# A convolution worked by halves: channel tile 7 moved from ScalarE and GpSimd to TensorE and VectorE, two row spreads merged, and two more filling matmuls

## The chip, the cores and the metric

The kernel runs on one core of a Trainium2 chip. A core has TensorE (PE in the profile) for matrix products, VectorE (DVE), ScalarE (ACT) and GpSimd (POOL) for elementwise work, and SyncE (SP), whose queue issues the DMA transfers. The metric is the device time of one execution in microseconds (us); lower is better. Three runs of the kernel before took 1380.88, 1380.84 and 1377.91 us, the median is 1380.84.

## The reference

Four layers work on x of 256 positions by 1024 channels (float32). Each adds a mixer and then a squared-ReLU MLP, both behind an RMS norm. The mixers are retention (layers 0 and 3), a convolution module (layer 1) and stick-breaking attention (layer 2). The change lies mostly in the convolution module:

```python
def conformer_conv_mixer(xn, pw1_w, pw1_b, dw_w, dw_b, ln_w, ln_b, pw2_w, pw2_b):
    h = xn @ pw1_w + pw1_b
    a, gate = jnp.split(h, 2, axis=-1)
    h = a * jax.nn.sigmoid(gate)
    h = lax.conv_general_dilated(          # depthwise, 31 taps, causal
        h, dw_w[:, None, :].astype(h.dtype), window_strides=(1,),
        padding=[(CONV_WIDTH - 1, 0)],
        dimension_numbers=('NWC', 'WIO', 'NWC'),
        feature_group_count=D_MODEL) + dw_b
    h = layer_norm(h, ln_w, ln_b)
    h = jax.nn.silu(h).astype(xn.dtype)
    return h @ pw2_w + pw2_b

for i in range(DEPTH):                      # DEPTH = 4
    h = rms_norm(x, norm_mix[i])
    x = x + mixer_i(h)
    x = x + squared_relu_mlp(rms_norm(x, norm_ffn[i]), ffn_w1[i], ffn_w2[i])
return rms_norm(x, final_norm)
```

## The kernel before

**Products.** Channels lie on the 128 partitions, positions along the free axis. A float32 product is made of three products of rounded values: every weight unit (128x1024) is loaded by SP into a raw buffer (L334), cast by ACT to its high part `wh` (L346), and VectorE subtracts to get the low part `wl` (L347). Activations are split in the same way. `mm_b` (L484 to L486), `mm_w` (L511, L512) and L552, L553 then multiply high by high, high by low and low by high. Outside the stretches named below a scheduler orders the instructions of each engine.

**Start.** `warm(9)` (L291) issues nine 128x512 matmuls on a tile of ones while the first weights are on their way. The first real matmul is L552, in retention.

**RMS norm.** The squares of four x tiles are added on GpSimd (L447). `norm_r` (L452ff) then lets GpSimd add the two halves of that sum (L455) into a new tile, TensorE sums over the channels (L393), VectorE makes a reciprocal root `r` in a chain of small operations (L377 to L388), and TensorE broadcasts it (L400).

**The convolution** (`conv`, L907ff). After pw1 and the gate, `hc[0..7]` holds the eight channel tiles, each 256 positions behind 31 zeros. The 31 taps of a tile are done in one of three ways:

- tile 0 on VectorE (`tap_dve`, L1004: one multiply-add per tap, into two accumulators that take turns, which lie in PSUM);
- tile 1 on ACT (a scaled copy, L1011) and GpSimd (an add, L1013);
- tiles 2 to 6 (`PET`) on TensorE. `spread` (L925) writes a tile's rows to DRAM (`hd`, L928) and reads them back (L931) so that four shifted copies of 32 channels fill the partitions. `taps_pe` (L1015) then needs 32 matmuls per tile and half, against diagonal weight strips that GpSimd prepares (L918). `spread(2)` and `spread(4)` move two tiles each, `spread(6, 1)` one.

Tile 7 is split by positions: its first half (`taps_7a`) is done on VectorE with accumulators in PSUM, its second half (`taps_7b`) on ACT and GpSimd.

From here the order on TensorE, VectorE, ACT and GpSimd is written out by hand (L1165 to L1250). A "half" h is 128 of the 256 positions. For each half: `fin_pe` (L1119) takes the convolution out of PSUM and subtracts a shift `Gb`, `square` (L1027) squares it on ACT, `stats` (L1035) sums over channels on TensorE, four tiles at a time; `cols_st` (L393), `mean_in`, `mean_out` (L410) and `scale_in` (a reciprocal root, L1058 to L388), `scale_out` (L410) make mean and scale; `swish_mean` (L1131), `swish` (L1136, then ACT's Silu, L1141 and L1142) normalise. The second product, pw2, has two parts. Channel tiles 0 to 3 are multiplied with unsplit weights `W` (L356 loads them, `mm_h`, L1159) half by half; tiles 4 to 7 are kept as high and low parts `y` (low part: L1146) and go through `mm_b` at the end. Then the MLP starts with L511.

On SP's queue the order around this is: the two spreads of tiles 2 to 5, the eight loads of `W` (L356, 256 KB each), the spread of tile 6 (L928, L931), and the loads of the next weights (L334), which wait for a raw buffer.

## Time and profile before

| | before |
|---|---|
| runs (us) | 1380.88, 1380.84, 1377.91; median 1380.84 |
| the profiled execution (us) | 1379.88, of which the span from first to last instruction is 1378.1 |
| granted TensorE clock, mean | 0.997 |
| TensorE busy | 1359.6 us (99%), weight loads 1233.6 us (90%) |
| VectorE, ScalarE, GpSimd busy | 985.8 us (72%), 784.1 us (57%), 146.3 us (11%) |
| DMA | 239.29 MB, mean 174 GB/s |

The profile is of one execution. A timeline row gives the start, the time from the first instruction's start to the last one's end, engine, line, operation, out<-in, the count, and in brackets the idle time before it and what ended it. Matmuls overlap, so the time from one matmul's start to the next one's is shorter than the time of one. A row of the waits gives, for what TensorE was about to start and what it waited for, total us, times, and the longest. A row of the windows gives busy time and count for each engine, then the granted clock as a share of full speed.

### The profile page before, as it was taken

The page shows a single profiled execution, that of the slowest core. Times are in us where ns is not written, and L with a number is a line of the kernel's source. Part 1 is how long each engine was busy: PE and PEld are TensorE (multiplying, and loading weights), DVE is VectorE, ACT ScalarE, POOL GpSimd, SP SyncE. Part 2 cuts the span into 40 slices and gives each one's busy share as a digit, 9 for nine tenths or more (in the row PEclk, how much of TensorE's full clock was granted, in tenths as well). Part 3 has the DMA queues.
Part 4 walks back from the last instruction along what each step waited for, and adds up shares of the span by engine and source line. Part 5 has one row for each costly group of instructions (what it writes and reads, how often), then busy time and mean ns, then how long its engine had stood idle before and what let it go on. Part 6 is the DMA issues. An engine that isn't in the chain of part 4 may idle for free.

```text
span 1378.1 us, 23268 instructions
## 1 busy us (share of the span) xinstructions
PE 1359.6 (99%) x9339; PEld 1233.6 (90%) x9339; DVE 985.8 (72%) x1709; ACT 784.1 (57%) x1203; POOL 146.3 (11%) x154
## 2 busy tenths in 40 slices
PE   9999999999999899999999999999999999999998
PEld 8889998888999798888988898888988999988888
DVE  6967778775679678765578587755597687788643
ACT  7555556664447567654468666644565554555442
POOL 2201003000218310000000010000120010100011
PEclk9999999999999999999999999999999999999999
DMA  7644446555556345555543345555454444455550
GB/s 288 217 153 154 153 154 214 184 184 187 180 184 158 128 148 195 189 190 188 187 157 123 137 169 184 186 190 199 171 181 175 153 154 165 173 191 190 190 190 34
DMA packets 38860, 239.29 MB, mean 174 GB/s; under 512 B 4320, under 2 KB 8160, under 8 KB 11360
## 3 DMA queue, kind: packets, MB, share of 16 engines
q1 hardware_dynamic: 38464, 237.28, 49.1%
q8 instruction: 73, 1.20, 0.3%
q10 hardware_dynamic: 288, 0.52, 0.1%
q14 instruction: 35, 0.29, 0.1%
HBM read 236.01 MB, written 1.78 MB: 173 GB/s over the span
## 4 chain that ended last, share of the span: by engine, by line
PE 94%; DVE 3%; ACT 2%; issue 1%; POOL 0%; DMA 0%; SPq 0%; ACTq 0%; DVEq 0%; POOLq 0%
PE acc L511 32%; PE acc L512 16%; PE acc L486 8%; PE acc L484 8%; PE acc L485 8%; PE acc L903 4%; PE acc L902 4%; PE acc L904 4%; DVE mis L1004 1%; PE acc L1159 1%; PE mis L393 1%; PE acc L500 1%; PE acc L498 1%; PE acc L499 1%; PE mis L400 1%; PE mis L799 1%
## 5 line engine op out<-in xcount | busy, mean ns | idle before, releaser
L347 DVE TENSOR_TENSOR wl<-raw,wh 128x1024 fp32r<-128x1024 f32 (+1 forms) x440 | 544.5, 1240 | 285.8 <-ACT wh L346 282.0
L346 ACT CAST wh<-raw 128x1024 fp32r<-128x1024 f32 (+1 forms) x440 | 456.7, 1041 | 422.2 <-PE acc L511 206.3
L511 PE MATMUL acc<-z,wh 128*128 128x512 f32 x1120 | 392.0, 395 | 0.0
L512 PE MATMUL acc<-z,wl 128*128 128x256 f32 x1120 | 312.9, 281 | 0.0
L511 PE MATMUL acc<-big,wh 128*128 128x512 f32 x768 | 269.0, 395 | 0.0
L511 PEld LDWEIGHTS acc<-z,wh 128*128 128x128 f32 x1120 | 209.4, 188 | 48.0
L512 PE MATMUL acc<-big,wl 128*128 128x256 f32 x768 | 215.4, 280 | 0.0
L512 PEld LDWEIGHTS acc<-z,wl 128*128 128x128 f32 x1120 | 211.5, 189 | 0.8
L511 PEld LDWEIGHTS acc<-big,wh 128*128 128x128 f32 x768 | 144.0, 187 | 33.8
L486 PE MATMUL acc<-big,wl 128*128 128x256 f32 x544 | 153.5, 283 | 0.0
L485 PE MATMUL acc<-big,wh 128*128 128x256 f32 x544 | 153.3, 283 | 0.0
L484 PE MATMUL acc<-big,wh 128*128 128x256 f32 x544 | 153.1, 284 | 0.0
L484 PE MATMUL acc<-z,wh 128*128 128x256 f32 x512 | 146.1, 286 | 0.0
L486 PE MATMUL acc<-z,wl 128*128 128x256 f32 x512 | 145.9, 285 | 0.0
L485 PE MATMUL acc<-z,wh 128*128 128x256 f32 x512 | 145.7, 285 | 0.0
L512 PEld LDWEIGHTS acc<-big,wl 128*128 128x128 f32 x768 | 145.1, 189 | 0.0
L447 POOL TENSOR_TENSOR t<-t,t 128x512 f32<-128x512 f32 x25 | 38.4, 1534 | 748.1 <-DVE z L432 458.8
L485 PEld LDWEIGHTS acc<-big,wh 128*128 128x128 f32 x544 | 104.2, 192 | 0.0
L486 PEld LDWEIGHTS acc<-big,wl 128*128 128x128 f32 x544 | 104.2, 192 | 0.0
L484 PEld LDWEIGHTS acc<-big,wh 128*128 128x128 f32 x544 | 103.6, 192 | 0.5 <-issue 0.3
L486 PEld LDWEIGHTS acc<-z,wl 128*128 128x128 f32 x512 | 98.8, 193 | 0.0
L484 PEld LDWEIGHTS acc<-z,wh 128*128 128x128 f32 x512 | 98.8, 193 | 0.0
(253 smaller groups left out, 1901.7 us busy)
## 6 DMA issues: line engine op xcount, KB each, us to landing
raw<-in_w SPq DMA_DIRECT2D x214, 1024.0 KB, 4.8
raw<-in_w SPq DMA_DIRECT2D x8, 512.0 KB, 8.0
raw<-hd SPq DMA_DIRECT2D x8, 263.0 KB, 4.7
x<-in_x SPq DMA_DIRECT2D x4, 256.0 KB, 6.3
big<-in_w SPq DMA_DIRECT2D x4, 256.0 KB, 6.2
t<-in_w SPq DMA_DIRECT2D x4, 256.0 KB, 7.6
cst<-in_cst SPq DMA_DIRECT2D x4, 192.0 KB, 5.0
hd<-big SPq DMA_DIRECT2D x5, 143.5 KB, 1.9
```

The lines of the kernel that those rows point to most:

```text
L346: nc.scalar.copy(hi[:, s], src[:, s])
L347: nc.vector.tensor_sub(lo[:, s], src[:, s], hi[:, s])
L393: return self.nc.tensor.matmul(dst, src, sc, start=start, stop=stop, skip_group_check=True)
L447: (nc.vector if p == 3 and self.quick else nc.gpsimd).tensor_add(a, self.sq, q)
L484: nc.tensor.matmul(o, wh[:, kk, cs], ah, start=st, stop=False, **kw)
L485: nc.tensor.matmul(o, wh[:, kk, cs], al, start=False, stop=False, **kw)
L486: nc.tensor.matmul(o, wl[:, kk, cs], ah, start=False, stop=en, **kw)
L511: nc.tensor.matmul(ps[m], wh[:, kk, cs], a, start=first and kk == 0, stop=False, **kw)
L512: nc.tensor.matmul(ps[m][:, :S], wl[:, kk, cs], a[:, :S], start=False, stop=last and kk == 3, **kw)
L902: nc.tensor.matmul(ps[t], zh[:, s], wh[:, kk], start=k == 0, stop=False, skip_group_check=True)
L903: nc.tensor.matmul(ps[t], zh[:, s], wl[:, kk], start=False, stop=False, skip_group_check=True)
L904: nc.tensor.matmul(ps[t], zl[:, s], wh[:, kk], start=False, stop=k == 7, skip_group_check=True)
```

## The change

1. `warm(9)` becomes `warm(11)`.
2. `norm_r` with `halves` adds in place instead of into a new tile. The scheduler places that add by itself.
3. `PET` takes tile 7 in. Tile 7's first half is done by `taps_pe(7, 0)` on TensorE, its second half by VectorE (`taps_7`, all 31 taps), with both accumulators in SBUF. ACT and GpSimd do no taps of tile 7 any more; GpSimd makes two more weight strips.
4. `spread` always moves two tiles: tiles 6 and 7 share one. The loads of `W` are issued behind that spread.
5. Hand order: `taps_pe(6, 0)` and `(7, 0)` stand behind `(3, 1)`; `shift_bb` stands one tile of taps later.
6. Mean and scale of both halves go into one tile each (`lnb`, `lnr`), so that tiles 4 to 7 are normalised once at full width, at the end (`swish_hl`), and no longer by halves.

The diff, cut to its core:

```diff
-PET = (2, 3, 4, 5, 6)
+PET = (2, 3, 4, 5, 6, 7)
...
-        self.warm(9)
+        self.warm(11)
...
         if halves:
-            sq, n = self.tmp(S), 1
-            nc.gpsimd.tensor_add(sq, self.sq[:, :S], self.sq[:, S:])
+            sq, n = sq[:, :S], 1
+            nc.gpsimd.tensor_add(sq, sq, self.sq[:, S:])
...
-        spread(6, 1)
+        sp = spread(6)
...
-        r7 = halves(self.mis(), P), halves(self.bigt(), P)
+        r7 = halves(self.bigt(), P)
...
-        def taps_7a(ws):
-            for w in ws:
-                tap_dve(7, w, r7[0][w % 2], w < 2, w == 0, 0)
-
-        def taps_7b(ws):
-            for w in ws:
-                tap_pool(7, w, r7[1][w % 2], w < 2, w == 0, 1)
...
+        def taps_7(ws):
+            for w in ws:
+                tap_dve(7, w, r7[w % 2], w < 2, w == 0, 1)
...
+        def swish_hl(*ds):
+            def hi(d):
+                y[d] = self.bigt(F32R)
+                return y[d][:, :S]
+
+            a = slice(0, S)
+            swish(a, ds[0], fn=hi)
             for d, e in zip(ds, ds[1:] + (None,)):
                 if e is not None:
-                    begin(e)
-                end(d)
+                    swish(a, e, fn=hi)
+                nc.vector.tensor_sub(y[d][:, S:], cc[d][:, a], y[d][:, a])
...
-            W = [self.unit_raw(key(0, p), [(self.tmp if p < 2 else self.bigt)() for _ in range(2)]) for p in range(4)]
             taps_pe(2, 0)
             shift_a()
...
             shift_c()
-            fin_pe(0, 2, 3, 4)
+            with self.tc.issue_after(sp.ins):
+                W = [self.unit_raw(key(0, p), [(self.tmp if p < 2 else self.bigt)() for _ in range(2)]) for p in range(4)]
+            fin_pe(0, 2, 3)
...
             taps_pe(6, 0)
+            taps_7(range(24, CW))
             fin_pe(0, 6)
+            taps_pe(7, 0)
+            fin_7()
+            fin_pe(0, 7)
             taps_pe(4, 1, range(4))
             stats(0, 4, 5, 6, 7)
...
-            swish_mean(0, 4, 5, 6, 7)
             fin_pe(1, 6)
-            swish(0, 4, 5)
...
-            swish(0, 6, 7)
...
             for p in range(4):
                 mm_h(p, range(4), 1)
-            swish_mean(1, 4, 5, 6, 7)
-            swish(1, 4, 5, 6, 7)
+            swish_mean(slice(0, S), 4, 5, 6, 7)
+            swish_hl(4, 5, 6, 7)
```

Where instructions move, by engine. A row is line, operation, out<-in, shape and what the instruction waits for; "x15" says that it stands so often.

GpSimd in the first retention layer, before. L447 are the adds of the squares, L455 is `norm_r`'s add, L727 fills a score tile after the Activation it waits for:

```order
L447 TENSOR_TENSOR t_33_269<-t_31_265,t_32_267 128x512 [waits Activation_49,Pool_49]
L727 TENSOR_TENSOR big_255<-t_37_278 128x256 [waits Activation_49]
L727 TENSOR_TENSOR big_356<-t_48_351 128x256 [waits Activation_49]
L727 TENSOR_TENSOR big_356<-t_60_425 128x256 [waits Activation_49]
L455 TENSOR_TENSOR t_74_504<-t_33_269 128x256 [waits DVE_49,Pool_49]
```

The same place after the change (line numbers are lower by one):

```order
L446 TENSOR_TENSOR t_33_271<-t_31_267,t_32_269 128x512 [waits Activation_49,Pool_49]
L454 TENSOR_TENSOR t_33_271<-t_33_271 128x256 [waits Pool_49]
L726 TENSOR_TENSOR big_257<-t_37_280 128x256 [waits Activation_49]
L726 TENSOR_TENSOR big_358<-t_48_353 128x256 [waits Activation_49]
L726 TENSOR_TENSOR big_358<-t_60_427 128x256 [waits Activation_49]
```

The add has moved ahead of three others, and it waits for GpSimd's own last add only, no longer for VectorE, which used to release the new tile.

TensorE in the convolution, before, from `taps_pe(3, 1)` to the second four tiles of `stats` of half 0 (`acc_4883` to `acc_4886` are the PSUM tiles, `raw_4865` holds the spread rows of tile 6, `cst` the ones for the sum):

```order
L1017 MATMUL acc_4884<-raw_4837,big_4282 32x128 x16
L1017 MATMUL acc_4883<-raw_4865,big_4292 32x128 [waits DMAHW6_49,DMAHW5_49,DMAHW7_49,DMAHW4_49,DVE_49]
L1017 MATMUL acc_4883<-raw_4865,big_4292 32x128 x15
L1017 MATMUL acc_4883<-raw_4865,big_4294 32x128 x16
L1017 MATMUL acc_4885<-raw_4845,big_4284 32x128 x16
L1035 MATMUL mis_5277<-big_4875,cst 32x256
L1035 MATMUL mis_5277<-big_4876,cst 32x256 [waits Activation_49]
L1035 MATMUL mis_5277<-big_4877,cst 32x256 [waits Activation_49]
L1035 MATMUL mis_5277<-big_4878,cst 32x256
```

And after (`raw_4870` holds the rows of tiles 6 and 7):

```order
L1017 MATMUL acc_4888<-raw_4841,big_4282 32x128 x16
L1017 MATMUL acc_4887<-raw_4870,big_4292 32x128 [waits DMAHW6_49,DMAHW5_49,DMAHW7_49,DMAHW0_49,DVE_49]
L1017 MATMUL acc_4887<-raw_4870,big_4292 32x128 x15
L1017 MATMUL acc_4887<-raw_4870,big_4294 32x128 x16
L1017 MATMUL acc_4888<-raw_4870,big_4296 32x128 [waits DVE_49]
L1017 MATMUL acc_4888<-raw_4870,big_4296 32x128 x15
L1017 MATMUL acc_4888<-raw_4870,big_4298 32x128 x16
L1017 MATMUL acc_4889<-raw_4849,big_4284 32x128 x16
L1036 MATMUL mis_5235<-big_4880,cst 32x256
L1036 MATMUL mis_5235<-big_4881,cst 32x256 [waits Activation_49]
L1036 MATMUL mis_5235<-big_4882,cst 32x256 [waits Activation_49]
L1036 MATMUL mis_5235<-big_4883,cst 32x256 [waits Activation_49]
```

32 matmuls for tile 7's first half stand between the taps of tile 6 and the sums; the sums still wait for ACT's squares of tiles 5, 6 and 7.

VectorE at the end of the convolution, before, behind the multiplications of half 1's first four tiles by its scale (`lnr`):

```order
L1136 TENSOR_TENSOR big_4874<-big_4874,lnr_963_5654 128x128 [waits DVE_49]
L347 TENSOR_TENSOR wl_5675<-raw_5622,wh_5674 128x1024 [waits Activation_49]
L1131 TENSOR_TENSOR big_4875<-big_4875,lnb_952_5606 128x128
L1131 TENSOR_TENSOR big_4878<-big_4878,lnb_952_5606 128x128 [waits Pool_49]
L347 TENSOR_TENSOR wl_5804<-raw_5801,wh_5803 128x1024 [waits DMAHW1_49,Activation_49]
L1136 TENSOR_TENSOR big_4875<-big_4875,lnr_963_5654 128x128 [waits DVE_49]
L347 TENSOR_TENSOR wl_5844<-raw_5801,wh_5843 128x1024 [waits Activation_49]
L347 TENSOR_TENSOR wl_5888<-raw_5885,wh_5887 128x1024 [waits DMAHW2_49,Activation_49]
L1146 TENSOR_TENSOR big_5573<-big_4875,big_5573 128x128 [waits Activation_49]
```

And after, from the same multiplication to the low part of tile 4 (L1146):

```order
L1127 TENSOR_TENSOR big_4879<-big_4879,lnr_4892 128x128 [waits DVE_49,Activation_49]
L347 TENSOR_TENSOR wl_5591<-raw_5588,wh_5590 128x1024 [waits DMAHW1_49,Activation_49]
L1121 TENSOR_TENSOR big_4880<-big_4880,lnb_4891 128x256
L1121 TENSOR_TENSOR big_4883<-big_4883,lnb_4891 128x256
L347 TENSOR_TENSOR wl_5686<-raw_5588,wh_5685 128x1024 [waits Activation_49]
L1127 TENSOR_TENSOR big_4880<-big_4880,lnr_4892 128x256 [waits DVE_49]
L347 TENSOR_TENSOR wl_5728<-raw_5725,wh_5727 128x1024 [waits DMAHW2_49,Activation_49]
L1127 TENSOR_TENSOR big_4881<-big_4881,lnr_4892 128x256 [waits DVE_49]
L347 TENSOR_TENSOR wl_5768<-raw_5725,wh_5767 128x1024 [waits Activation_49]
L347 TENSOR_TENSOR wl_5812<-raw_5809,wh_5811 128x1024 [waits DMAHW3_49,Activation_49]
L1146 TENSOR_TENSOR big_5631<-big_4880,big_5631 128x256 [waits Activation_49]
```

(The two middle L1131 and the two middle L1121 rows are left out.) Tiles 4 to 7 now pass at 256 columns, once, and five weight splits instead of four stand between the last scale and the first low part.

116 lines of the change are left out of this document (49 added, 67 removed).

## The prediction, before the run

> **What bounds the kernel now.** The page comes first: the span, the busy shares, and the chain that ended last.
>
> ```profile
> span 1378.1 us, 23268 instructions
> PE 1359.6 (99%) x9339; PEld 1233.6 (90%) x9339; DVE 985.8 (72%) x1709; ACT 784.1 (57%) x1203; POOL 146.3 (11%) x154
> PE 94%; DVE 3%; ACT 2%; issue 1%; POOL 0%; DMA 0%; SPq 0%; ACTq 0%; DVEq 0%; POOLq 0%
> ```
>
> TensorE is the path: 94% of the chain lies on it. So time is won only where TensorE waits, runs at a lower clock, or has less to do, and each matmul that is added costs its own length. The second view is therefore everything that TensorE waited for, over the whole run (what it was about to start, what it waited for, us in total, times, the longest).
>
> ```profile
> PE mis L1035 <- ACT big L1027: 3.5, 2, 2.3
> PE acc L1159 <- ACT big L1142: 1.9, 1, 1.9
> PE mis L393 <- POOL t L455: 1.6, 1, 1.6
> PE acc L1017 <- DMA raw<-hd: 1.4, 1, 1.4
> PE mis L291 <- POOL ones L269: 1.3, 1, 1.3
> PE acc L552 <- ACT wh L346: 0.9, 1, 0.9
> PE mis L400 <- DVE lns L1085: 0.8, 1, 0.8
> PE mis L410 <- DVE vy L388: 0.6, 1, 0.6
> PE acc L1017 <- issue: 0.3, 1, 0.3
> ```
>
> The list is short, and the change touches nearly all of it. Six rows belong to the convolution: 3.5 + 1.9 + 1.4 + 0.8 + 0.6 + 0.3 = 8.5 us. One belongs to `norm_r` (1.6), one to the start (0.9). Nothing else in 1378 us waits, so whatever is won early is carried to the end: no wait on other engines is there to take it back, unless a new one arises.
>
> The third view is the clock, in windows around the long waits.
>
> ```profile
> 40.00:60.00 20.00, 18.40 (x133) 17.82 (x132) 20.00 (x33) 10.48 (x17) 6.23 (x5) 0.91 0.54 189
> 44.00:48.00 4.00, 4.00 (x23) 4.00 (x22) 4.00 (x6) 2.27 (x4) 1.40 (x2) 0.58 0.76 295
> 480.00:490.00 10.00, 8.11 (x58) 7.91 (x57) 6.45 (x21) 7.92 (x14) 0.00 (x0) 0.83 0.15 43
> ```
>
> The seventh figure of a row, behind the five busy times, is the granted clock. Of 4 us at 0.58, (1 - 0.58) x 4 = 1.7 us of clock are missing; of 10 us at 0.83, also 1.7. At half clock that is 3.4 us each, once behind the 1.6 us wait for L455 and once behind the 1.9 us wait for L1142. So each of these two waits cost its own length and 1.7 us more.
>
> **Start: two more fillers.** The timeline of TensorE, and ACT's cast of the second weights:
>
> ```profile
> 1.29 4.02 PE L291 MATMUL mis<-ones 128*128 128x512 bf16 x9 [1.29 <-POOL ones L269]
> 6.24 1.22 PE L552 MATMUL acc<-z,wh 128*128 128x512 f32 x2 [0.92 <-ACT wh L346]
> 8.96 1.05 PE L552 MATMUL acc<-z,wh 128*128 128x512 f32 x2
> 11.07 0.62 PE L552 MATMUL acc<-z,wh 128*128 128x512 f32 x2
> 13.86 0.63 PE L552 MATMUL acc<-z,wh 128*128 128x512 f32 x2
> 9.36 1.14 ACT L346 CAST wh<-raw 128x512 fp32r<-128x512 f32 x2 [0.64 <-DMA raw<-in_w]
> ```
>
> A filler takes 4.02 / 9 = 0.45 us. Two take 0.9 and end at 5.31 + 0.9 = 6.2, where the first cast ends: the 0.92 us of idle cover them. If that cover were shorter in some run, they would cost up to 0.9.
>
> What they may bring is the clock. A group of products takes 8.96 - 6.24 = 2.7 us at first and (13.86 - 11.07) / 2 = 1.4 later, so full clock came between 8.96 and 11.07. If it is granted in a fixed beat of 3.4 us, then counting ten beats back from the drop near 44.6 (44.6 - 34.1) gives 10.5 for that moment, and the beat before began at 7.1. The idle 0.92 us lies in the beat from 3.7 to 7.1; with it filled, full clock should come at 7.1. Then the weights bound: their cast starts at 9.36, its first half is there at 9.36 + 0.57 = 9.9, and the group at 11.07 can start 1.1 us earlier. I take 1.1; ends: -0.9 (late first matmul), +1.7 (a whole beat).
>
> **The norm's add.** GpSimd did it at 41.84; the sums follow, and much later the root is broadcast:
>
> ```profile
> 41.84 1.57 POOL L455 TENSOR_TENSOR t<-t 128x256 f32<-128x256 f32 x1 [3.10 <-DVE big L740]
> 43.47 0.61 PE L393 MATMUL mis<-cst,t 128*128 128x1 f32 x4 [1.60 <-POOL t L455]
> 65.28 0.16 DVE L388 SCALAR_TENSOR_TENSOR ry<-rt,ry 128x2 f32<-128x2 f32 x1
> 68.99 0.60 PE L400 MATMUL mis<-cst,ry 128*128 128x128 f32 x4
> ```
>
> GpSimd stood idle 3.10 us before the add: what released it was VectorE (L740), since the new tile's old content had to be read first. In place, and placed behind the last add of squares, it needs neither, and TensorE finds it done. The wait (1.6) and the half-clock stretch (1.7) go: 3.3 us. What is late next is VectorE, which is busy in all 20.00 of 20 us from 40 to 60 and can't come forward with TensorE. Its root ends at 65.44, TensorE uses it at 68.99: a margin of 3.55 us, against 1.1 + 3.3 = 4.4 wanted. VectorE gains part of the first 1.1 itself, so I lose a third of a microsecond: 3.0. Ends: 0 (VectorE gives all of it back) and 3.5.
>
> **The convolution.** The stretch runs from the first taps to the start of pw2's second part (L484), which is unchanged itself.
>
> ```profile
> 441.52 1.96 PE L1017 MATMUL acc<-raw,big 128*32 128x128 f32 x64
> 457.25 2.84 PE L1017 MATMUL acc<-raw,big 128*32 128x128 f32 x96 [1.43 <-DMA raw<-hd]
> 489.34 3.74 PE L1159 MATMUL acc<-big,big 128*128 128x128 f32 x32
> 492.83 0.72 PE L484 MATMUL acc<-big,wh 128*128 128x256 f32 x4
> ```
>
> It lasts 492.83 - 441.52 = 51.3 us. Less 8.5 of waits and 1.7 of clock, 41.1 are work and the refilling of the pipeline behind waits, Two rows of taps give both prices: 96 records in 2.84 and 64 in 1.96, so (2.84 - 1.96) / 32 = 0.0275 a record, and 0.2 from the last start to its end, which I take, as an estimate, for the refill behind each of seven waits. Added is one half of a tile: 32 matmuls, 64 records, 1.8 us. Sums, broadcasts and L1159 keep their number. So the work is 41.1 - 1.0 + 1.8 = 41.9, if five of the seven refills go. Which waits stay?
>
> *Tile 6's rows* (1.4) and the W loads. SP's queue, and three rows of the page on DMA (the last figure is the median from issue to landing):
>
> ```profile
> 445.14 0.33 SPq L928 DMA_DIRECT2D hd<-big  x1
> 451.65 1.75 SPq L931 DMA_DIRECT2D raw<-hd  x4
> raw<-hd SPq DMA_DIRECT2D x8, 263.0 KB, 4.7
> t<-in_w SPq DMA_DIRECT2D x4, 256.0 KB, 7.6
> hd<-big SPq DMA_DIRECT2D x5, 143.5 KB, 1.9
> ```
>
> The row write was issued at 445.14, behind the W loads, and the read back only at 451.65, 6.5 us later; the write's usual time is 1.9. With W behind, the writes go out as the gate's last product ends (L953, below: 443.82 + 0.87 = 444.7), the read back near 446.6 to 448.4, and the rows land by 453. TensorE reaches tile 6 after six halves (10.6) and 1.5 of sums and broadcasts, near 453.6. Moved past on SP's queue are two writes and four reads; W then goes out from about 448 and lands by 461, while the first L1159 comes near 466. This wait goes, with 5 us to spare for W.
>
> *The shift* (0.8 and the 0.3 next to it): its broadcast stands a tile of taps later, 1.8 us against 1.1. Gone.
>
> *The squares of half 0's second four* (2.35): VectorE was the slow one, with 31 taps of tile 7 on the way to tile 7's square.
>
> ```profile
> 453.49 2.70 DVE L1004 SCALAR_TENSOR_TENSOR mis<-big,prm,mis 128x128 f32<-128x128 f32 x7
> 456.10 0.35 DVE L1119 SCALAR_TENSOR_TENSOR big<-acc,prm,Gb 128x128 f32<-128x128 f32 x1
> 469.23 0.60 DVE L1119 SCALAR_TENSOR_TENSOR big<-acc,prm,Gb 128x128 f32<-128x128 f32 x2
> 443.82 0.87 DVE L953 SCALAR_TENSOR_TENSOR big<-t,prm,t 128x256 f32<-128x256 f32 x2
> ```
>
> A tap in PSUM takes (456.10 - 453.49) / 7 = 0.37 to 0.39 us. No row shows one of this width with both operands in SBUF: L1119, one in PSUM, stands at 0.30 or less a piece, and the SBUF form at 256 columns at 0.87 / 2 = 0.43, so 0.26 to 0.30. I take 0.28, next to L1119, the row of the same width. From the shift, ready near 448.5, VectorE owes seven L1119 (2.1), tile 0 (0.8), 25 taps (7.0) and tile 7's finish (0.6): 459.0; ACT's square adds 0.4. TensorE gets there after 1.8 us more taps, near 458.4. About 1.0 us of wait stays. With taps at 0.39 it would be 3.8.
>
> *Half 1's squares* (1.1) wait for tile 5 alone now, not for ACT's taps: 0.3 stays. *The root's broadcast* (0.6) sits behind VectorE's chain with GpSimd silent: gone.
>
> *The swish* (1.9): ACT's swish of tiles 0 to 3 of half 1 no longer stands behind those of tiles 6 and 7. Gone, and the 1.7 of clock with it.
>
> *A new wait.* The low part of tile 4 now stands on VectorE behind five weight splits.
>
> ```profile
> 478.73 1.23 DVE L347 TENSOR_TENSOR wl<-raw,wh 128x1024 fp32r<-128x1024 f32 x1 [0.39 <-ACT wh L346]
> 479.87 0.89 DVE L1131 TENSOR_TENSOR big<-big,lnb 128x128 f32<-128x128 f32 x4
> ```
>
> From the scale of half 1 VectorE owes four L1136 like these (0.9), five splits (5 x 1.15 from start to start), four subtractions and two multiplications of double width (6 x 0.35), one low part and its waits for ACT's two swishes of tile 4: about 10 to 11.5. TensorE owes rather more than half of pw2's first part, (492.83 - 489.34) / 32 a record: 5.75 of the eight groups of 16, 92 records, 10.0, and the first four L484, 0.5. I put a wait of 0.8 there, between 0 and 1.3.
>
> So the stretch is 41.9 + 1.0 + 0.3 = 43.2, with the new wait 44.0; before 51.3. That is 7.3. Counted instruction by instruction along TensorE's new order, with taps at 1.76 a half, the same stretch is some 1.5 shorter, since waits let me count too much as work. I take 8.0, between 4.5 (slow taps, 1.3 behind L1146) and 9.5.
>
> **The clock gate.** The rows above show half clock after idle times of 1.6 and 1.9 us, and none after 1.4 and 2.35: length alone doesn't decide. I count no drop behind the waits that stay, of 1.0 or less. [...]
>
> **Sum.** 1.1 + 3.0 + 8.0 = 12.1. The profiled execution took 1379.88, so 1367.8; it lies 0.96 below the median of 1380.84, so against that median 1368.7, say 1368.5. A measurement of this kernel can tell about 0.3%, 4.1 us, from no change.
>
> **Rivals.**
>
> - *Taps no faster in SBUF.* Each tap reads the accumulator written two taps before; if that sets the pace, 0.39 stays. For it: PSUM taps run at 0.37 to 0.39 though L1119 takes 0.30. Against: the SBUF rows. The wait for the squares becomes 3.8: 1371.3. Chance 0.12.
> - *VectorE takes the norm's gain back.* For it: 20.00 busy of 20. Against: the margin of 3.55. Then 1371.5. Chance 0.12.
> - *The two drops of the clock stay*, as something other than the gaps makes them: +3.4, 1371.9. Against: both follow a gap at once, and no other is on record in the middle of the run. Chance 0.04.
> - *The waits only move.* VectorE's part is as long as before, TensorE has 1.8 more to do, and the norm's gain is lost: 1380.84 + 1.8 - 1.1, near 1381. Against: two of the waits, the rows (1.4) and the swish (1.9), have a cause of their own that goes. Chance 0.05.
> - *W late, slower.* Place: the first L1159. The loads of W are behind the spread, and stand in line with the next weights. Each microsecond that W lands after 466 costs one; it undoes the gain at 12.1 late and is 0.3% slower at 16.2, so with a landing near 482, 34 us after issue. They needed 7.6. Chance 0.02.
> - *All waits gone* and a better start: 1363.5. Chance 0.05.
>
> **How the numbers follow.** The forecast has 0.60, on its own 1365 to 1371.5. The range has to take in the first three rivals and the full gain: 1363 to 1374. Faster by more than 0.3% (below 1376.7): 0.60 + 0.12 + 0.12 + 0.04 + 0.05 = 0.93. Within: 0.05. Slower: 0.02.
>
> **What would show it.** In the changed kernel's waits, no row for the norm's add, none for raw<-hd, none for L1142's successor; a row of about 1.0 for the sums behind ACT's square, one near 0.8 at L484 or L485. Windows from 44 to 48 and around the end of the convolution at 1.00; the third group of the start near 10.0. The taps on VectorE at 0.28 from start to start. From the first taps to the first matmul of pw2's second part, about 43. I am wrong if the time is over 1374: then either VectorE sets the pace (waits on VectorE between 45 and 70, or a square wait over 3), or W does.

## The result and the profile after

The changed kernel takes 1369.46 us (median of 4 runs, 1369.21 to 1372.64) against 1380.86 before (4 runs, 1377.91 to 1381.38). The ratio is 0.9927, 95% interval 0.9907 to 0.9947: 11.4 us less. The forecast was 1368.5, with a range of 1363 to 1374. The profiled execution took 1369.21, its span is 1367.4 against 1378.1: 10.7 us less.

The page of the changed kernel, first the span and the busy times, then one row of the DMA queues that will matter:

```profile
span 1367.4 us, 23303 instructions
PE 1354.1 (99%) x9405; PEld 1227.7 (90%) x9405; DVE 983.8 (72%) x1698; ACT 771.1 (56%) x1164; POOL 138.3 (10%) x125
...
q8 instruction: 73, 1.20, 0.3%
```

What TensorE waited for, over the whole run (columns as before; "issue" is time in which the engine waited for nothing that the profile shows):

```profile
PE acc L1017 <- issue: 2.0, 2, 1.7
PE mis L291 <- POOL ones L269: 1.3, 1, 1.3
PE acc L1017 <- DVE big L1004: 1.2, 1, 1.2
PE acc L484 <- DVE big L1146: 1.1, 1, 1.1
PE acc L551 <- ACT wh L346: 1.1, 2, 0.7
PE acc L510 <- DVE z L431: 0.8, 2, 0.4
```

Of the nine rows of before, the norm's add, the swish, the squares, the shift and the root are gone. Two that the forecast struck out are there in a new shape: the stop called issue has grown from 0.3 to 2.0, and there is 1.2 ahead of tile 6. The windows around the old long waits, now at full clock (the seventh figure):

```profile
40.00:60.00 20.00, 20.00 (x145) 18.93 (x144) 20.00 (x35) 11.67 (x18) 5.92 (x4) 1.00 0.52 184
44.00:48.00 4.00, 4.00 (x36) 4.00 (x35) 4.00 (x8) 1.78 (x3) 1.03 (x1) 1.00 0.72 287
480.00:490.00 10.00, 8.86 (x75) 8.65 (x74) 5.28 (x10) 4.10 (x7) 0.00 (x0) 1.00 0.59 211
```

From here the run is cut at three landmarks in the timeline: the first taps, the first L484 product (`mm_b` of pw2; L483 after the change) and the first product of the MLP behind it.

| us | before | after | gained |
|---|---|---|---|
| start to first taps | 441.52 | 437.38 | 4.14 |
| first taps to `mm_b` | 51.31 | 44.24 | 7.07 |
| `mm_b` to the MLP | 11.61 | 12.99 | -1.38 |
| MLP to the end of the span | 873.62 | 872.82 | 0.80 |
| span | 1378.06 | 1367.43 | 10.63 |

**Start and norm.** The timeline of TensorE: the fillers, the first, third and fifth group of products, and the broadcast of the root:

```profile
1.30 4.87 PE L291 MATMUL mis<-ones 128*128 128x512 bf16 x11 [1.30 <-POOL ones L269]
6.52 0.73 PE L551 MATMUL acc<-z,wh 128*128 128x512 f32 x2 [0.35 <-ACT wh L346]
...
10.29 0.73 PE L551 MATMUL acc<-z,wh 128*128 128x512 f32 x2 [0.70 <-ACT wh L346]
...
13.17 0.63 PE L551 MATMUL acc<-z,wh 128*128 128x512 f32 x2
...
64.72 0.66 PE L400 MATMUL mis<-cst,ry 128*128 128x128 f32 x4
```

The third group starts 0.8 earlier (11.07 before), held by the cast, as the 0.70 in brackets says. GpSimd's add now follows its last add of squares at once:

```profile
28.11 1.84 POOL L446 TENSOR_TENSOR t<-t,t 128x512 f32<-128x512 f32 x1 [0.40 <-ACT t L441]
30.03 1.61 POOL L454 TENSOR_TENSOR t<-t 128x256 f32<-128x256 f32 x1
```

It is done at 31.6, and VectorE ends the root at 64.62 by the trace, TensorE takes it at 64.72: the margin of 3.55 us was used up to the last tenth, and not overdrawn.

**The convolution**, TensorE:

```profile
437.38 1.96 PE L1017 MATMUL acc<-raw,big 128*32 128x128 f32 x64
...
451.22 1.08 PE L1017 MATMUL acc<-raw,big 128*32 128x128 f32 x31 [1.22 <-DVE big L1004]
452.63 3.71 PE L1017 MATMUL acc<-raw,big 128*32 128x128 f32 x128 [0.33 <-issue]
458.00 0.30 PE L1017 MATMUL acc<-raw,big 128*32 128x128 f32 x1 [1.66 <-issue]
458.00 0.72 PE L1036 MATMUL mis<-big,cst 128*32 128x256 f32 x8
...
481.62 0.72 PE L483 MATMUL acc<-big,wh 128*128 128x256 f32 x4
483.48 0.39 PE L484 MATMUL acc<-big,wh 128*128 128x256 f32 x1 [1.14 <-DVE big L1146]
```

The 1.22 is put down to VectorE's L1004, which wrote tile 7's accumulator and has nothing to do with it. SP's queue shows the true cause:

```profile
440.36 1.02 SPq L927 DMA_DIRECT2D hd<-big  x2
443.33 2.71 SPq L930 DMA_DIRECT2D raw<-hd  x4
446.14 1.82 SPq L356 DMA_DIRECT2D t<-in_w  x4
...
452.78 46.60 SPq L334 DMA_DIRECT2D raw<-in_w  x7
```

The four reads landed at 446.55, 448.21, 449.58 and 451.13 by the trace, and TensorE went on at 451.22. The 1.66 stands ahead of one last tap, the 160th record since 451.22, not ahead of the sums: the sums would have waited for ACT's squares, but the last of those had ended at 456.28. VectorE was early:

```profile
448.02 1.66 DVE L1004 SCALAR_TENSOR_TENSOR big<-big,prm,big 128x128 f32<-128x128 f32 x6
449.59 0.35 DVE L1112 SCALAR_TENSOR_TENSOR big<-acc,prm,Gb 128x128 f32<-128x128 f32 x1
...
455.59 0.35 DVE L1112 SCALAR_TENSOR_TENSOR big<-acc,prm,Gb 128x128 f32<-128x128 f32 x1 [0.87 <-PE acc L1017]
...
480.74 2.35 DVE L347 TENSOR_TENSOR wl<-raw,wh 128x1024 fp32r<-128x1024 f32 x2
483.01 0.42 DVE L1146 TENSOR_TENSOR big<-big,big 128x256 fp32r<-128x256 f32 x1
```

Six taps take 449.59 - 448.02 = 1.57, 0.26 each, and at tile 7 VectorE waits for TensorE. At the end the low part of tile 4 stands behind the splits as forecast; TensorE waits 1.14.

**What the stop called issue is.** The page counts 9405 matmuls and 9405 weight loads on TensorE, 18810 instructions, and 73 transfers of 16 KB on the queue of kind instruction: 18810 / 73 = 258 to a transfer, on the mean, which is called a block here. Counted from TensorE's first instruction, the stop of 0.31 in the kernel before was at number 6337, those of the changed kernel at 6850 and 7106. The last two are 256 apart, and divided by 256 the three leave 193, 194 and 194 (a record may be missing from a trace): each stop is read as the border of a block. The block that TensorE waited for at 458.00 was moved from 455.53 to 456.64 by the trace. The taps use up 256 instructions in 3.7 us (443.28 - 439.55, two transfers of blocks in the quiet part), faster than any other stretch of this kernel; `mm_b`, at 0.12 us for a matmul and its load, needs 15. At these three stops TensorE went on 1.36, 1.47 and 1.36 us after a block had landed (449.04 - 447.68 before, 452.63 - 451.16 and 458.00 - 456.64 after the change); in the other kernels profiled here it was 1.2 to 1.5 at the stops called issue among the taps.

### The profile page after: what moved, and what is told of

Its sections match the earlier page's. It is cut to its first block, busy times and chain, and to the rows that moved or that the text cites. A ratio compares the mean times of both kernels' runs of the same rounds, so it can differ in the third digit from the quotient of the medians.

```text
span 1367.4 us, 23303 instructions
## 1 busy us (share of the span) xinstructions
PE 1354.1 (99%) x9405; PEld 1227.7 (90%) x9405; DVE 983.8 (72%) x1698; ACT 771.1 (56%) x1164; POOL 138.3 (10%) x125
## 4 chain that ended last, share of the span: by engine, by line
PE 96%; DVE 2%; DMA 1%; issue 0%; ACT 0%; SPq 0%; DVEq 0%; ACTq 0%
PE acc L510 32%; PE acc L511 16%; PE acc L485 9%; PE acc L483 9%; PE acc L484 9%; PE acc L901 4%; PE acc L902 4%; PE acc L903 4%; PE acc L1017 1%; PE mis L393 1%; DVE wl L347 1%; PE acc L499 1%; PE acc L497 1%; PE acc L498 1%; PE mis L400 1%; PE mis L798 1%
## 5 line engine op out<-in xcount | busy, mean ns | idle before, releaser
L510 PEld LDWEIGHTS acc<-z,wh 128*128 128x128 f32 x1120 | 209.3, 188 | 49.6 <-DVE z L431 1.5
L511 PEld LDWEIGHTS acc<-z,wl 128*128 128x128 f32 x1120 | 210.9, 188 | 1.0
L484 PE MATMUL acc<-big,wh 128*128 128x256 f32 x544 | 153.4, 283 | 1.1 <-DVE big L1146 1.1
L483 PE MATMUL acc<-big,wh 128*128 128x256 f32 x544 | 153.0, 284 | 0.0
L483 PE MATMUL acc<-z,wh 128*128 128x256 f32 x512 | 145.5, 285 | 0.0
L484 PE MATMUL acc<-z,wh 128*128 128x256 f32 x512 | 144.9, 283 | 0.0
L484 PEld LDWEIGHTS acc<-big,wh 128*128 128x128 f32 x544 | 104.3, 192 | 1.4 <-DVE big L1146 1.4
L483 PEld LDWEIGHTS acc<-big,wh 128*128 128x128 f32 x544 | 103.7, 192 | 0.5 <-issue 0.3
L484 PEld LDWEIGHTS acc<-z,wh 128*128 128x128 f32 x512 | 98.1, 192 | 0.0
L483 PEld LDWEIGHTS acc<-z,wh 128*128 128x128 f32 x512 | 98.1, 192 | 0.0
```

The source lines that it names most:

```text
L483: nc.tensor.matmul(o, wh[:, kk, cs], ah, start=st, stop=False, **kw)
L484: nc.tensor.matmul(o, wh[:, kk, cs], al, start=False, stop=False, **kw)
L510: nc.tensor.matmul(ps[m], wh[:, kk, cs], a, start=first and kk == 0, stop=False, **kw)
L511: nc.tensor.matmul(ps[m][:, :S], wl[:, kk, cs], a[:, :S], start=False, stop=last and kk == 3, **kw)
```

## The experiments

Theory: the gain is the sum of three parts that don't touch each other (start 0.7, norm 3.4, convolution 5.7 and a little behind it), and the convolution fell 2.3 short of the forecast because TensorE ran out of instructions and the rows came late. Rivals: the norm's gain is given back by VectorE; the stop ahead of the sums is a wait for data.

The ratios are to new runs of the kernel before beside each group (median 1379.77 for E1 to E4, 1379.65 for E5 to E8, 1380.77 for E9 to E12). Their intervals reach 1.5 to 2.9 us to either side, so what one variant of the changed kernel does differently from another is read mostly from the profiles.

**E1, the two edits outside the convolution alone** (kernel before).

```diff
-        self.warm(9)
+        self.warm(11)
...
-            sq, n = self.tmp(S), 1
-            nc.gpsimd.tensor_add(sq, self.sq[:, :S], self.sq[:, S:])
+            sq, n = sq[:, :S], 1
+            nc.gpsimd.tensor_add(sq, sq, self.sq[:, S:])
```

> The kernel before with the two edits outside the convolution alone: 11 fillers, and norm_r adding in place. Theory (the parts add up): the convolution is entered about 4.1 us earlier, as in the changed kernel (437.4 against 441.5), and nothing is given back: about 1376.7, a gain of 4.1. The wait for L455 and the half-clock stretch from 44.6 to 48.0 are gone; the waits of the convolution stay at 8.5 us. Rival (VectorE takes the norm's gain back): a new wait on VectorE between 45 and 70 us, and a gain of 0.7 to 1.1.

1376.33 (10 runs), ratio 0.9978 (0.9967 to 0.9989): 3.0 less by the ratio, where 4.1 were expected, which the interval allows. In the profiled run the first taps start at 437.13, 4.4 earlier, and no row in the waits stands between 20 and 440 us: nothing is given back. The profiled run, 1374.76, says more. It has the same wait of 1.90 for the swish as the kernel before, and no half clock behind it:

```profile
479.60 0.60 PE L1159 MATMUL acc<-big,t 128*128 128x128 f32 x3 [1.90 <-ACT big L1142]
```

```profile
474.00:486.00 12.00, 10.11 (x91) 9.91 (x90) 8.16 (x22) 8.60 (x16) 0.00 (x0) 1.00 0.18 48
```

The same 12 us of the kernel before:

```profile
478.40:490.40 12.00, 10.11 (x76) 9.91 (x75) 8.12 (x22) 8.59 (x16) 0.00 (x0) 0.86 0.16 51
```

Busy times agree to 0.04 us; only the clock differs, 1.00 and 0.86, and with it the stretch from the taps to `mm_b`, 49.64 against 51.31. So the 1.7 us behind this wait is a matter of chance, and so are some of the 3 to 5 us by which runs of one kernel differ: of the 18 runs of the kernel before that belong to E1 to E4, the seven with a mean granted clock of 0.997 to 0.999 took 1376.92 to 1378.47, the eleven with 0.995 or 0.996 took 1379.11 to 1381.65.

**E2, the convolution alone.**

```diff
-        self.warm(11)
+        self.warm(9)
...
-            sq, n = sq[:, :S], 1
-            nc.gpsimd.tensor_add(sq, sq, self.sq[:, S:])
+            sq, n = self.tmp(S), 1
+            nc.gpsimd.tensor_add(sq, self.sq[:, :S], self.sq[:, S:])
```

> The changed kernel with 9 fillers and norm_r's add in a new tile again, so that the convolution's part stands alone. Theory (parts add up): gain 5.7 in the convolution and 0.5 behind it, about 1374.7; the wait for L455 is back (1.6) and with it, in the profiled run, perhaps the half-clock stretch (1.7). Rival (the convolution's gain was due to entering it earlier, against transfers that keep their time): the stretch from the first taps to the first matmul of the MLP takes another length than the 57.2 us of the changed kernel by more than 1 us.

1373.72 (9 runs), ratio 0.9956 (0.9943 to 0.9969): 6.1 less, where 6.2 were expected. With E1's, 0.9978 x 0.9956 = 0.9934, against 0.9927 for the whole: the parts add up. From the taps to the MLP it takes 43.97 + 12.99 = 56.96 (57.23 in the changed kernel) though entered 4.2 us later: no transfer holds it. The wait for L454 is back with 1.6 and the half clock too:

```profile
44.00:48.00 4.00, 4.00 (x23) 4.00 (x23) 4.00 (x7) 2.27 (x4) 1.42 (x2) 0.57 0.75 289
```

**E3, the norm's add in a new tile** (changed kernel).

```diff
-            sq, n = sq[:, :S], 1
-            nc.gpsimd.tensor_add(sq, sq, self.sq[:, S:])
+            sq, n = self.tmp(S), 1
+            nc.gpsimd.tensor_add(sq, self.sq[:, :S], self.sq[:, S:])
```

> The changed kernel with norm_r's add in a new tile again, all else as changed. Theory: the scheduler puts the add back behind three others on GpSimd, TensorE waits 1.6 us for it, and the clock is halved for 3.4 us: 3.3 us slower than the changed kernel, about 1372.8. If the clock does not drop behind it this time: 1.6, about 1371.1. Rival (the add's place is worth nothing, since VectorE sets the pace there): within 0.5 of the changed kernel.

1370.43 (4 runs), ratio 0.9933 (0.9915 to 0.9951), 1.0 above the changed kernel's median. The profiled run shows the wait, GpSimd released by VectorE again, but of 0.9 us, since full clock came as late as 10.7 here and TensorE reached the place later:

```profile
43.42 1.04 POOL L454 TENSOR_TENSOR t<-t 128x256 f32<-128x256 f32 x1 [4.24 <-DVE big L739]
```

After 0.9 us the clock did not drop. By the times alone, 1.0 is not told apart from nothing. E2 and E4 (below) differ in this add alone, both with 9 fillers: the first taps start at 441.59 in E2, with the drop of the clock, and at 438.10 in E4, 3.5 earlier. So the place of the add is worth from 0.9 (the wait here) to 3.5 us, by how early TensorE comes and whether the clock falls.

**E4, 9 fillers** (changed kernel).

```diff
-        self.warm(11)
+        self.warm(9)
```

> The changed kernel with 9 fillers. Theory: an idle gap of about 0.9 us is back ahead of the first real matmul, full clock comes later, and the third group of products starts near 11.1 instead of 10.3: 0.7 slower, about 1370.2. Rival (full clock comes at a moment of the chip's own, whatever the fillers do): full clock anywhere between 6.4 and 10.5, and a time between 1369.5 and 1370.2 by chance.

1369.55 (4 runs), ratio 0.9925 (0.9908 to 0.9942): no difference in the median. In the profile the first taps start at 438.10 instead of 437.38, 0.7 later, as expected; 0.7 is 0.05% of the time, less than the runs can tell. By the trace's record of the clock, full clock came at 9.97, 10.50 and 10.57 in the three profiled runs with 9 fillers, and with 11 at 4.0 to 7.3 in nine and at 10.69 in one (E3). So with 11 fillers it came earlier in nine of ten runs, not in all.

This profile and E2's also say something of the stop ahead of the sums. With 9 fillers there are four TensorE instructions fewer ahead of it, a border stands a matmul or two later in the program, and the stop is no longer at the last tap but at the sums themselves (L1036), at the same number beyond a multiple of 256:

```profile
PE mis L1036 <- issue: 2.1, 1, 2.1
```

**E5, short fillers**, to move the borders of the blocks.

```diff
-        for _ in range(n):
+        for _ in range(4 * n):
...
-                self.nc.tensor.matmul(ps, self.ones[:, :P], self.ones, start=True, stop=True, skip_group_check=True)
+                self.nc.tensor.matmul(ps[:, :P], self.ones[:, :P], self.ones[:, :P], start=True, stop=True, skip_group_check=True)
```

> The changed kernel with its 11 fillers of 512 columns cut into 44 of 128: the same filling time, but 33 more matmuls and weight loads, 66 TensorE instructions, ahead of everything. Theory (TensorE ran out of instructions, which arrive in blocks of 256): both stops that the profile calls issue were at instruction 193 of a block of 256; all block borders move 66 instructions ahead in the program, to about the point where TensorE waits for the rows of tiles 6 and 7, so that the 1.7 us stop ahead of the sums is gone or moved to another instruction, 0.9 us of taps earlier: 1.5 to 2 us faster, about 1367.7. Rival (the stop ahead of the sums is a wait for ACT's squares or for a transfer): it stays ahead of the same instruction, 1.7 us long, and the time within 0.5 of the changed kernel.

1370.66 (4 runs), ratio 0.9932 (0.9915 to 0.9949): not faster. But the stops moved as the theory said:

```profile
449.74 1.16 PE L1017 MATMUL acc<-raw,big 128*32 128x128 f32 x35
453.44 3.95 PE L1017 MATMUL acc<-raw,big 128*32 128x128 f32 x127 [2.53 <-issue]
458.19 1.17 PE L1017 MATMUL acc<-raw,big 128*32 128x128 f32 x33 [0.81 <-issue]
459.11 0.39 PE L1036 MATMUL mis<-big,cst 128*32 128x256 f32 x3
```

They are at numbers 6850 and 7106 again, which are other matmuls now: the second stands 33 tap records ahead of the sums, no longer one. A wait for data would have stayed where it was. What the theory got wrong is the price: the first stop, now at the rows of tile 6, took 2.53 in place of their 1.22. Its block was moved from 451.11 to 452.03 only, behind the rows and W. Here the moved border moved the late block with it and did not bring it earlier.

**E6, W early.**

```diff
+        W = []
+
+        def w_early(q):
+            u = PLAN.index(("conv_pw2_w", j, "b", 0, q * 256))
+            W.append([(self.tmp if q < 2 else self.bigt)() for _ in range(2)])
+            for i, t in enumerate(W[q]):
+                o = u % UPC * 1024 + i * 512
+                nc.sync.dma_start(t, self.w_d[u // UPC][:, o : o + 512])
+
         for p in range(1, 4):
+            for q in ((0,), (1, 2), (3,))[p - 1]:
+                w_early(q)
...
-            with self.tc.issue_after(sp.ins):
-                W = [self.unit_raw(key(0, p), [(self.tmp if p < 2 else self.bigt)() for _ in range(2)]) for p in range(4)]
+            self.un += 4
```

> The changed kernel with the loads of W taken out from behind the last spread and issued one to three column pairs earlier, during the first product, where the DMA engines are half idle. Theory (the W loads delay TensorE's instruction blocks and the rows of tiles 6 and 7): the stops called issue shrink from 2.0 to under 0.7, the rows' wait from 1.2 to about 0.7: 1.5 to 2.5 faster, about 1367.4. Rival (instruction blocks come late by themselves, since taps use them up faster than they come): the stops stay, and the time within 0.5 of the changed kernel. Second rival (early W takes the place of the next weights): new waits on wh between 410 and 440.

1368.35 (4 runs), ratio 0.9914 (0.9897 to 0.9931). The rows' wait fell to 0.38, the taps to `mm_b` take 42.94 instead of 44.24. The stop remained at 1.38:

```profile
456.91 0.30 PE L1028 MATMUL acc<-raw,big 128*32 128x128 f32 x1 [1.38 <-issue]
```

In the waits the stops fell from 2.0 to 1.4, half of what was expected: some for the theory, some for its rival. But in those 5 us the DMA engines (the figure before the last) were 45% busy all the same, with the next megabyte of weights, which now went out earlier, at 450.3:

```profile
451.80:456.90 5.10, 3.71 (x128) 3.44 (x128) 3.14 (x12) 1.24 (x4) 0.00 (x0) 1.00 0.45 182
```

That is the mean; in the 2.9 us from the border to the start of the next block (451.80 to 454.69) they were 78% busy. E10 tells theory and rival apart.

**E7, the low part of tile 4 on GpSimd.**

```diff
-                nc.vector.tensor_sub(y[d][:, S:], cc[d][:, a], y[d][:, a])
+                (nc.gpsimd if d == 4 else nc.vector).tensor_sub(y[d][:, S:], cc[d][:, a], y[d][:, a])
```

> The changed kernel with the low part of tile 4 subtracted by GpSimd, idle there, in place of VectorE, where it stands behind five weight splits. Theory: the wait of 1.1 us behind L1146 goes, with 0.2 for refilling: 1.3 faster at the end of the convolution, about 1368.2, unless VectorE's chain at the MLP's start takes some of it back (it made TensorE wait 0.8 there). Rival (the low parts of tiles 5 to 7 are as late): the wait moves to the next one, within 0.3 of the changed kernel.

1373.85 (5 runs), ratio 0.9954 (0.9937 to 0.9972), 4.4 above the changed kernel's median. The subtraction that VectorE does in 0.42 took GpSimd 4.32:

```profile
482.66 4.32 POOL L1146 TENSOR_TENSOR big<-big,big 128x256 fp32r<-128x256 f32 x1 [37.38 <-ACT big L1131]
```

VectorE was busy for 3.7 of those 4.3 us, 2.4 of them in two weight splits. TensorE waited 2.7 for it and 3.0 for z behind it, and the stretch from `mm_b` to the MLP takes 16.32 instead of 12.99. The profiled run also has a stop of 2.5 for instructions, behind which the clock fell to half (the run's mean is 0.998, against 0.999 in the changed kernel); it stands at 458.34, ahead of the moved subtraction, so the 2.1 us by which the stretch from the taps to `mm_b` is longer there are not put down to this edit. Both theory and rival miss: the wait did not move, it grew.

**E8, tile 7's accumulators in PSUM.**

```diff
-        r7 = halves(self.bigt(), P)
+        r7 = halves(self.mis(), P)
```

> The changed kernel with tile 7's two accumulators in PSUM, as before the change. Theory: a tap takes 0.37 to 0.39 again instead of 0.26; 25 taps behind the shift are 2.8 us longer, VectorE waited 1.1 us for TensorE in that stretch, and the stop for instructions ahead of the sums covers 1.7 more: 0 to 1 us slower, up to 1370.5. Rival (the pace of a tap is set by the accumulator it depends on, in whichever memory): the same 0.26 and the same time.

1369.99 (4 runs), ratio 0.993 (0.9911 to 0.9948). The taps are as slow as before the change:

```profile
448.95 2.31 DVE L1004 SCALAR_TENSOR_TENSOR mis<-big,prm,mis 128x128 f32<-128x128 f32 x6
451.16 0.34 DVE L1112 SCALAR_TENSOR_TENSOR big<-acc,prm,Gb 128x128 f32<-128x128 f32 x1
```

(451.16 - 448.95) / 6 = 0.37 against 0.26, in the same order of instructions: the memory makes the difference, and the rival is out. Whether the dependence has a part in either pace is not shown. It costs next to nothing, since the tap that TensorE stops at comes late anyway: the stop fell to 0.9 while waits for VectorE rose to 1.7.

**E9, W ahead of the last spread again.**

```diff
-        sp = spread(6)
+        for q in range(4):
+            w_early(q)
+        sp = spread(6)
```

> The changed kernel with one part of the change undone: the eight loads of W stand on SP's queue ahead of the spread of tiles 6 and 7 again, as in the kernel before. Theory (the rows' arrival bounds this place): the row write goes out about 4 us later and shares the engines with W, the rows land 4 to 7 us later than in the changed kernel (451.1), and TensorE waits 5 to 8 us for them instead of 1.2; the stop for instructions ahead of the sums hides behind that wait in part: 2.5 to 6 slower, about 1373.5. Rival (the place of the W loads does not matter): within 0.5 of the changed kernel.

(With `w_early` as in E6, called here alone.) 1370.12 (4 runs), ratio 0.9929 (0.9912 to 0.9946): 0.7 above the changed kernel's median, 0.3 by the ratios, so no difference that these runs can tell, where 2.5 to 6 were expected. The rows landed at 452.93 instead of 451.13, and TensorE waited only 0.6 for them, because it had lost 2.16 before:

```profile
445.08 0.85 PE L1028 MATMUL acc<-raw,big 128*32 128x128 f32 x20 [2.16 <-issue]
```

This is the border ahead of those of the changed kernel, number 6338. In either place of W the longest stop stands at a border, 2.16 here and 1.66 in the changed kernel; which border it was went with the place of W.

**E10, W early and the next weights late.**

```diff
+    def load_chunk(self, un, eng):
+        t = self.raw.tile([P, RAWW], F32, name=self.nm("raw"), tag="raw")
+        n = 1024 if un < 4 * UPC else UPC * 1024
+        for o in range(0, UPC * 1024, n):
+            eng.dma_start(t[:, o : o + n], self.w_d[un // UPC][:, o : o + n])
+        return t
...
-                self.rawt = self.raw.tile([P, RAWW], F32, name=self.nm("raw"), tag="raw")
...
+                self.rawt = self.pre.pop(self.un, None) or self.load_chunk(self.un, nc.sync)
...
             stats_out(0)
+            self.pre[self.un] = self.load_chunk(self.un, nc.scalar)
```

> The kernel with the early W loads, and the next megabyte of weights, which went out at 450.3 and landed at 455.2, asked for on ACT's queue only behind the copy of half 0's sums, near 458. So almost nothing but TensorE's instructions moves between 450.6 and 458. Theory (the instruction block comes late because the DMA engines are busy with weights when it is asked for): it starts about 1 us after the border instead of 2.9, and the stop at the next border shrinks from 1.4 to 0.3 or less: about 1367.0. Rival (a block takes 5 us from border to use whatever else moves): the stop stays at 1.4, and the time at 1368.3.

1366.86 (4 runs), ratio 0.9908 (0.9893 to 0.9923), as expected; E6 has 0.9914, which the times alone don't tell from it. The changed kernel between the two stops, with the same two figures last:

```profile
452.70:458.00 5.30, 3.64 (x128) 3.37 (x128) 2.10 (x8) 0.93 (x3) 0.00 (x0) 1.00 1.02 390
```

E10 there:

```profile
452.10:456.10 4.00, 3.71 (x130) 3.44 (x130) 2.56 (x10) 0.93 (x3) 0.00 (x0) 1.00 0.01 4
```

and its stop, 0.29 instead of 1.66:

```profile
456.10 0.30 PE L1033 MATMUL acc<-raw,big 128*32 128x128 f32 x1 [0.29 <-issue]
```

From border to border it is 5.4 us with the engines full, 5.1 with them at 45%, 4.0 with them idle; the taps need 3.7. By the trace the next block began to move 2.90 us after the border in the changed kernel, with the engines full (2.4 to 3.8 in E2, E4, E5 and E7, full there too), 2.89 in E6, and 1.69 here, where 1 had been expected; with the engines idle it was 1.11 in E12 and 1.10 in E9, behind its stop at 445.08. So the theory holds, if with a longer start: without the weights on the engines the block began to move 2.90 - 1.69 = 1.2 us sooner. A stop of 0.3 stays with the engines idle.

**E11, a weight split behind tiles 4 and 5.**

```diff
-            W1 = [self.unit(key(1, 0))]
             for p in range(4):
                 mm_h(p, range(4), 1)
             swish_mean(slice(0, S), 4, 5, 6, 7)
-            swish_hl(4, 5, 6, 7)
+            swish_hl(4, 5)
+            W1 = [self.unit(key(1, 0))]
+            swish_hl(6, 7)
```

> The changed kernel with the first weight split of pw2's second part (ACT's cast and VectorE's subtraction) put behind the swish and low parts of tiles 4 and 5, where it stood ahead of all of them. Theory: the low part of tile 4 is ready near 477 instead of 483.4, TensorE does not wait behind L484 any more: 1.1 + 0.2 faster, about 1368.1. Rival (VectorE or ACT owes as much in total, so that the wait goes to a weight split or to the low part of tile 6): another wait of 0.5 to 1.5 between 482 and 490, and no gain.

1371.83 (4 runs, 1369.71 to 1373.82), ratio 0.9943 (0.9922 to 0.9964). The wait behind L1146 is gone, `mm_b` to the MLP takes 11.60 instead of 12.99. It came back at the MLP, later than the rival had put it: TensorE waits 1.9 there for VectorE's z (L431), at 498.08, and the clock falls behind it:

```profile
494.00:504.00 10.00, 7.77 (x33) 6.12 (x33) 10.00 (x13) 5.76 (x10) 4.70 (x4) 0.83 0.39 144
```

VectorE is busy 10.00 of 10 us. It is what bounds the passage from pw2 to the MLP here; the order in it chose the place of the wait.

**E12, E6, E10 and E11 together.**

> Early W loads, the later weight chunk and the moved weight split together. Theory (the parts add up): 1.1 + 1.4 + 1.3 faster than the changed kernel, about 1365.7, with the stretch from the first taps to the first matmul of the MLP at 53.5 instead of 57.2. Rival (a wait that one edit takes away turns up behind another): 1367 or more.

1368.21 (4 runs), ratio 0.9918 (0.9903 to 0.9932). The stretch from the taps to the MLP is 41.57 + 11.60 = 53.2, as hoped, but the wait of 1.9 at the MLP and the half clock behind it (a mean of 0.998, against 0.999 in E10) are here too: the rival's case.

```profile
PE acc L515 <- DVE z L436: 1.9, 1, 1.9
```

E10 has the lowest time of all that were run, 0.9908 against the changed kernel's 0.9927, though the intervals overlap.

## Why the prediction was right, point by point

- **The bound.** TensorE is the path, and the forecast that early gains are carried to the end held: 4.14 at the first taps, 9.83 at the MLP, 10.6 at the end.
- **Start**, 1.1 forecast, 0.7 measured (E4). The mechanism held in the profiled run: the idle 0.92 covered all but 0.3 of the fillers (the first product starts at 6.52 instead of 6.24), and full clock came earlier, 6.42 instead of 10.50. The cast of the second weights then bound it, a little later than the sum had it: the third group at 10.29, not near 10.0.
- **The norm's add**, 3.0 forecast, 4.14 - 0.7 = 3.4 measured (3.5 between E2 and E4), of which 1.7 only when the clock would have dropped (E3). VectorE did not take it back (E1): it ended its root early enough, by a tenth.
- **The convolution**, 8.0 forecast, 5.7 measured (7.07 - 1.38). This is the term that was mis-sized, in two steps. "This wait goes", of tile 6's rows: it kept 1.22. The reads went out 0.9 later than expected, and took 7.8 us from the first issue to the last landing; the sum used the page's median of one read, 4.7, from the last issue. The four come in one after the other, 1.4 to 1.7 apart. And "Gone", of the 0.3 called issue: the row was in the list, was taken for a part of the wait beside it, and is the first sign of what then cost 2.0. Against that, neither the 1.0 for half 0's squares nor the 0.3 for half 1's was needed.
- **The choice of 8.0** over the 7.3 that the waits gave went away from the result, though its reason held. Less its waits of 3.2, the stretch to `mm_b` has 44.24 - 3.2 = 41.0 of work, not 41.9. What the instruction-by-instruction count had no place for is the stop, which the kernel before barely shows.
- **Taps in SBUF**, 0.28 forecast, 0.26 measured; the rival of 0.39 is refuted by E8, which puts it back by the memory alone.
- **The new wait** behind the splits, 0.8 forecast, 1.14 measured. That VectorE bounds the whole passage, so that 0.8 more is lost at the MLP (the waits' last row), was missed; E11 shows that it is one and the same.
- **The clock.** 1.66 us without a drop in the changed kernel, 1.60 with one before: that length alone does not decide was right. The rival that the drops have a cause of their own is out: all six half-clock stretches between the start and the end of the 14 profiled runs stand behind an idle time, of 1.60 and 1.90 us in the kernel before, 1.6 in E2, 2.5 in E7, 1.9 in E11 and in E12; they left with the waits, and came back behind others.
- **W late**: W landed at 457.44, TensorE used it from 465.96. The rival never came near. That W would hurt by delaying instructions was on no list.
- **The total** came out closer than its parts, and that is in part luck: the sum was 12.1, the profiled span fell by 10.6 and the medians by 11.4. Against the convolution's 2.3 too much stand the norm's 0.4 and 0.8 behind the MLP, which no term had; and the two drops of the clock, 3.4 of the sum, were in the profiled execution of before, but not in every run of that kernel (E1).

What stays open: how much of the 0.8 us gained behind the MLP belongs to which place, and what exactly decides the drop of the clock. Nor did any run undo the edits inside the convolution one by one, other than the accumulators' memory (E8) and the place of W (E9): that the other edits took away the waits they were meant for is read from the rows of the waits, not shown by a run.

## What to carry to other kernels

The taps, 256 instructions in 3.7 us, outpaced the transfers of their own instructions: where a row called issue appears in the waits, count TensorE's instructions from stop to stop (256 in the changed kernel), and try the stretch without bulk transfers (E10: 1.66 to 0.29). A wait that is put down to an engine long done can be a transfer (the 1.22 us put down to L1004 were one); look up its landing before believing the name. And when a wait is pushed off an engine that is busy all the time, look for it behind the next consumer before counting the gain (E11: 1.14 gone at L1146, 1.9 at the MLP).

## What the runs showed of the hardware

- **Instruction blocks.** The stops called issue among the taps stood at 6337 in the kernel before and at 6850 and 7106 in the changed kernel, 193 or 194 beyond a multiple of 256, and at 6850 and 7106 again in E5, where those were other matmuls. They ended 1.36, 1.47 and 1.36 us after a block had landed (before and after the change; 1.2 to 1.5 in the other runs). The block began to move 2.90 us after the border before it in the changed kernel, with the DMA engines full (2.4 to 3.8 in E2, E4, E5 and E7), and 1.69 in E10, with them idle (1.10 in E9, 1.11 in E12).
- **The clock.** In the kernel before, the granted clock was 0.50 from 44.64 to 48.05 and from 484.96 to 488.37, for 3.41 us each time, behind idle times of 1.60 and 1.90 us. Its changes at 10.50, 44.64, 48.05, 484.96 and 488.37 are 10, 1, 128 and 1 times 3.413 us apart. The windows of E2 (0.57 of 4 us) and E11 (0.83 of 10 us) miss 1.7 us of clock each, as before the change, behind 1.6 and 1.9 us. No half clock followed 1.43 and 2.35 us in the kernel before, 1.22 and 1.66 in the changed kernel, 1.90 in E1, 2.1 in E4 and 2.53 in E5. So length alone did not decide; what did is not shown.
- **GpSimd beside VectorE.** In E7 a subtraction of 128x256 took GpSimd 4.32 us beside VectorE's weight splits, two multiplications and low parts, ten times VectorE's own 0.42; beside VectorE's reads of PSUM it did a subtraction of that size in 0.74 (L1092 in the changed kernel). It is one instance, and the output's type differs (fp32r, f32), so the cause is not shown.
